# Second-half weights of the attention output projection loaded during attention, into closed tiles' place; row buffers and odd heads' raw query weights share tags

## The chip, the cores and the metric

The kernel runs on one core of one Trainium2 chip. Its engines work at the same time, each through its own instructions in a fixed order, and wait for one another by semaphores: TensorE (PE in the profile; its weight loads PEld), VectorE (DVE), ScalarE (ACT), GpSimd (POOL) and SyncE (SP), which issues most DMA transfers. The metric is the device time of one launch in microseconds.

Before the change the time is 2666.85 us (median of 3 runs, 2663.87 to 2669.19). All stretches below are microseconds from the start of the span of one profiled execution.

## What is computed

One inference step of a two-layer decoder in float32: model width 1024, one prompt of 1024 tokens, and 8 decode sequences of 8 tokens ("samples"). Layer 0 is an S5 state-space mixer and a gated convolutional feed-forward net. Then one shared K and V is projected. Layer 1 is differential attention over it and a second feed-forward net. The part in question:

```
xn = rmsnorm(x, b_pre_g)
q  = (xn @ w_q).reshape(seq, 8 heads, 2, 64)
S_j = softmax(q[:, h, j] @ k[:, h, j].T / 8 + ALiBi bias(h), causal)   # j = 0, 1
o[:, h] = rmsnorm((S_0 - lam * S_1) @ v[:, h], sub_g) * const
x  = x + rmsnorm(o @ w_o, b_post_g)
x  = x + rmsnorm(conv_ffn(rmsnorm(x, f_pre_g)), f_post_g)
```

The samples attend to their own paged past as well. Their scores and values are worked off beside the K and V projection, and their outputs go to a scratch tensor `sod` in device memory.

## The kernel before

Every large product runs in three matmuls: each float32 operand is split into a high and a low part in a fast format, and high*high, low*high and high*low are accumulated (`mm3`, lines 815, 816, 817). A weight is loaded raw by DMA, cast to its high part on ACT (line 798 for the general weights, 1812 for the query weights), and the low part is raw minus high, on DVE (line 799) or POOL (line 1813). An activation is transposed on PE and split by ACT and DVE on the way out of PSUM (lines 150 to 154).

The stages follow one another: S5, its gated output, feed-forward net 0, K/V projection with the samples' attention (`kv_proj`, until about 1462), attention (until about 1801), output projection (`o_proj`, until about 1889) and feed-forward net 1 (to the end). A scheduler orders each engine's instructions over the borders of stages from a model of their times; what is written first does not always come first. Tiles live in pools. A pool that opens where another has closed reuses its bytes, and the first instruction that writes such a tile waits for all instructions that used the old tiles under it.

`attention` has eight heads. `prep(h)` prepares a head: it loads `raw`, the head's 1024x128 piece of w_q (tag `qraw`, one buffer), and `kr`, its keys; multiplies `raw` by the norm's gain on POOL (line 1811), casts it to `qwh` on ACT, subtracts to `qwl` on POOL; makes the bias tile `tb`; transposes the keys into `kh` and `kl` (64 partitions, copied to the other 64 by DMAs that POOL issues, lines 1826 and 1827); and runs 48 matmuls of 512 columns for the queries `qx`. For head 0 the loads of `raw` and `kr` are issued by POOL, for the others by SP. `prep(0)` runs ahead of the loop; the other heads' steps are spread over the loop by the table `STEPS`. In the loop `stage_a` makes scores (lines 1904, 1905), maxima (1907) and exponentials (1911), and `stage_b` combines the two maps (1921), transposes (1929), multiplies by the values (1935) and normalises.

During the last head the rows of `o` come back from scratch (`row_in`, tags `kr` and `row` in turn), are completed with the two last heads' outputs (line 1866), transposed (`row_T`, line 876), and the first half of w_o's columns is multiplied for five of the nine token tiles (`o_half`), with weights in the query and key tiles of even heads. Then `o_proj` loads the second half in four units of 512 KB (`half_units`, `load_w`, lines 793, 798, 799), multiplies it for all nine token tiles (the samples' tile needs the cast at line 976 and uses lines 989, 990), then the first half for the four late tiles. Each finished tile goes through a norm and residual tail (lines 845, 857, 860, 870) that feeds feed-forward net 1.

Of the kernel before, what the change touches and what calls it, by code (L numbers as in the profile page):

```python
# [20 lines left out]
P = 128  # L21
D = 1024
# [51 lines left out]
def trunk_kernel(ctx, tc, I, O):  # L74
# [7 lines left out]
    def nm(s):  # L82
        uid[0] += 1
        return f"{s}_{uid[0]}"
# [679 lines left out]

    def open_w():

        pools["w"] = wstack.enter_context(tc.tile_pool(name="wpool", bufs=1, reuse_waits="tile"))

    def open_dense():

        if "w" not in pools:
            open_w()
        pools["ph"] = wstack.enter_context(tc.tile_pool(name="phase", bufs=1, reuse_waits="tile"))
# [7 lines left out]
    def wslot(name, dtype=F32):  # L781

        c = pools["wc"] = (pools.get("wc", -1) + 1) % NWX
        return pools["w"].tile([P, 1024], dtype, tag=f"wx{c}", name=nm(name), bufs=1)

# [206 lines left out]

    def half_units(wsrc, half, gains=lambda k2: None):
        wv = wsrc.rearrange("(kt p) f -> p kt f", p=P)
        u3 = lambda t: t.rearrange("p (k f) -> p k f", f=512)
        hs = slice(half * 512, half * 512 + 512)
        units = []
        for k2 in range(KT // 2):
            hi, lo = load_w([(u3, wv[:, 2 * k2 : 2 * k2 + 2, hs])], gains(k2))
            units.append((u3(hi), u3(lo)))  # L1000
        return units
# [767 lines left out]
    def attention():  # L1769
        with ExitStack() as ca:  # L1770
            ap1 = ca.enter_context(tc.tile_pool(name="att1", bufs=1, reuse_waits="tile"))
            ap = ca.enter_context(tc.tile_pool(name="att", bufs=1, reuse_waits="tile"))

            def at(shape, tag, bufs=1, dtype=F32, pool=None):
                return (pool or ap).tile(shape, dtype, tag=tag, name=nm(tag), bufs=bufs)
# [20 lines left out]
            def prep(h):  # L1796
# [3 lines left out]
                e = h % 2  # L1800
                raw = at([P, KT, P], "qraw")
                wh = at([P, KT, P], "qwh", 1, F32R)
# [4 lines left out]
                H.update(kh=kh, kl=kl, qx=qx)  # L1807
                dma = (nc.sync if h else GP).dma_start
                dma(raw, wq[:, :, hc])
                dma(kr, kd[0:SEQ, hc].rearrange("(n p) e -> p n e", p=P))  # L1810
                GP.tensor_tensor(raw, raw, bc(bpgc, 2, P), ALU.mult)
# [36 lines left out]
            def row_in(tt):  # L1848

                t0, n = tokens(tt)  # L1850
                t = rows[tt] = at([P, D], ("kr", "row")[tt % 2])
                if tt < NTT:
                    nc.sync.dma_start(t[:, 0 : D - 2 * P], od[t0 : t0 + n, 0 : D - 2 * P])
                    return
                for b in range(NB):

                    src = sod[b].rearrange("(c r) (g e) -> r g c e", r=40, g=2)[0:NQ]
                    dst = t[b * NQ : (b + 1) * NQ].rearrange("q (g c e) -> q g c e", g=2, c=4)
                    for g in range(2):
                        nc.sync.dma_start(dst[:, g], src[:, g])  # L1860
# [102 lines left out]
            for n in range(-LA, len(items)):  # L1963
# [18 lines left out]
                if n == (NH - 1) * NTT:  # L1982
                    row_in(NTT)
                    row_in(NTT - 1)
                if h < NH - 1:
                    stage_b(h, i, *live.pop(n))
                elif i == NTT - 1:
                    row_T(NTT)
                    row_in(i - 1)
                    stage_b(h, i, *live.pop(n))  # L1990
                else:
# [6 lines left out]
                    row_T(i + 1)  # L1998
                    if i:
                        row_in(i - 1)  # L2000
            o_half(1, us, None)
# [4 lines left out]
    def o_proj():  # L2006

        ws = half_units(I["w_o"][0], 1)
        post = row_bcast(I["b_post_g"][0])
# [103 lines left out]
```

## Time and profile before

| | |
|---|---|
| time, median of 3 | 2666.85 us (2663.87 to 2669.19) |
| profiled execution: its time, its span | 2665.99 us, 2664.1 us |
| mean granted TensorE clock | 0.98 of full speed |
| PE busy | 2493.7 us, 94% of the span |
| DVE busy | 1947.8 us, 73% |
| ACT busy | 1281.0 us, 48% |
| POOL busy | 661.2 us, 25% |
| chain that ended last | PE 58%, DVE 13%, DMA 4%, issue 4%, ACT 3%, POOL 3% |

A row of the profile names start, duration, engine (a q behind it marks the engine's DMA or semaphore queue), line, operation, output and inputs, and in brackets how long the engine had stood idle just before and what released it. Here PE is busy nearly everywhere, so what matters are the few places where PE stands idle, or where its granted clock is down after standing.

### The profile page before, as it was taken

What the parts mean: (1) busy time and instruction counts of PE and PEld (TensorE: products, weight loads), DVE (VectorE), ACT (ScalarE), POOL (GpSimd) and SP (SyncE); (2) the same over time, 40 slices, a digit from 0 to 9 for tenths busy, and PEclk for the clock granted to TensorE, in tenths of its full rate; (3) what the DMA queues carried; (4) which work ended last, traced back from release to release, by engine and by line L of the source; (5) the groups of instructions that cost most, each with busy time, mean ns of one, the idle gap of its engine ahead of it and who ended that gap; (6) DMA issues with size and microseconds to landing.
All of it is one profiled execution on the core that took longest, in us unless ns stands there. A gap on an engine that the chain in (4) does not pass through costs nothing.

```text
span 2664.1 us, 39516 instructions
## 1 busy us (share of the span) xinstructions
PE 2493.7 (94%) x14234; PEld 2199.5 (83%) x14234; DVE 1947.8 (73%) x3543; ACT 1281.0 (48%) x2597; POOL 661.2 (25%) x1062
## 2 busy tenths in 40 slices
PE   3778998999999999999999899999899999998997
PEld 2777876999999977788777788877799999996776
DVE  7994358677777789984222688875877777778999
ACT  6763234444444454354322677764544444444433
POOL 3220030111111176501201222113011111127571
PEclk9999998999999999999999899999899999999999
DMA  5443233122222233445646333325322222233334
GB/s 144 104 97 88 84 126 126 58 76 78 85 72 78 81 117 97 125 134 183 207 158 210 104 83 96 98 93 173 127 69 79 75 75 74 75 98 105 92 107 154
DMA packets 265688, 286.77 MB, mean 108 GB/s; under 512 B 42268, under 2 KB 212564, under 8 KB 265492
## 3 DMA queue, kind: packets, MB, share of 16 engines
q1 hardware_dynamic: 261892, 273.55, 33.3%
q0 software_dynamic: 3088, 9.77, 1.7%
q8 instruction: 113, 1.85, 0.3%
q10 hardware_dynamic: 512, 0.92, 0.1%
q14 instruction: 83, 0.68, 0.1%
HBM read 193.58 MB, written 70.93 MB: 99 GB/s over the span
## 4 chain that ended last, share of the span: by engine, by line
PE 58%; DVE 13%; DMA 4%; issue 4%; ACT 3%; POOL 3%; SPq 0%; DVEq 0%; ACTq 0%; POOLq 0%
PE mm L815 17%; PE mm L817 17%; PE mm L816 17%; DVE acc L1437 2%; PE mm L1426 2%; DVE xT_lo L151 2%; DMA gr<-gd 2%; DVE S L1907 1%; ACT S L1911 1%; DVE xT_hi L151 1%; DVE wst L151 1%; PE mm L1935 1%; PE tr L876 1%; DVE acc L860 1%; POOL xr L1306 1%
## 5 line engine op out<-in xcount | busy, mean ns | idle before, releaser
L815 PE MATMUL mm<-xT_hi,whi 128*128 128x384 f32 (+1 forms) x1408 | 457.0, 325 | 2.0 <-ACT acc L1154 1.7
L816 PE MATMUL mm<-xT_lo,whi 128*128 128x384 f32 (+1 forms) x1408 | 456.2, 324 | 1.4 <-DVE xT_lo L151 1.4
L817 PE MATMUL mm<-xT_hi,wlo 128*128 128x384 f32 (+1 forms) x1408 | 454.0, 324 | 0.0
L815 PEld LDWEIGHTS mm<-xT_hi,whi 128*128 128x128 f32 x1408 | 265.4, 189 | 3.8 <-ACT acc L1154 2.4
L816 PEld LDWEIGHTS mm<-xT_lo,whi 128*128 128x128 f32 x1408 | 265.7, 189 | 2.2 <-DVE xT_lo L151 2.1
L817 PEld LDWEIGHTS mm<-xT_hi,wlo 128*128 128x128 f32 x1408 | 265.3, 189 | 0.8
L1203 POOL COPY cvo<-acc 128x2 f32<-128x2 f32 x88 | 54.2, 616 | 814.1 <-ACT acc L1186 814.0
L815 PE MATMUL mm<-whi,xT_hi 128*128 128x512 f32 x608 | 242.9, 404 | 5.8 <-ACT whi L798 5.8
L1200 DVE SCALAR_TENSOR_TENSOR acc<-acc,cpar,acc 128x1104 f32<-128x1104 f32 x176 | 239.9, 1385 | 4.7 <-ACT acc L1198 4.7
L816 PE MATMUL mm<-wlo,xT_hi 128*128 128x512 f32 x608 | 242.8, 400 | 0.1
L817 PE MATMUL mm<-whi,xT_lo 128*128 128x512 f32 x608 | 242.2, 400 | 0.0
L150 ACT CAST whi<-raw 128x1024 fp32r<-128x1024 f32 x88 | 92.7, 1053 | 248.5 <-PE mm L817 245.1
L1437 DVE TENSOR_TENSOR acc<-mm,acc 128x512 f32<-128x512 f32 x279 | 184.3, 679 | 8.4 <-PE mm L817 8.1
L151 DVE TENSOR_TENSOR wlo<-raw,whi 128x1024 fp32r<-128x1024 f32 x88 | 107.7, 1224 | 103.5 <-PE mm L816 90.8
L815 PE MATMUL mm<-acc,whi 128*128 128x384 f32 x528 | 178.8, 339 | 2.5 <-DVE acc L1160 2.5
L817 PE MATMUL mm<-acc,wlo 128*128 128x384 f32 x528 | 178.9, 339 | 0.0
L816 PE MATMUL mm<-acc,whi 128*128 128x384 f32 x528 | 178.3, 338 | 0.0
L815 PEld LDWEIGHTS mm<-whi,xT_hi 128*128 128x128 f32 x608 | 115.3, 190 | 36.9 <-ACT whi L798 6.2
L816 PEld LDWEIGHTS mm<-wlo,xT_hi 128*128 128x128 f32 x608 | 115.2, 189 | 27.9 <-DVE wlo L799 0.8
L817 PEld LDWEIGHTS mm<-whi,xT_lo 128*128 128x128 f32 x608 | 114.9, 189 | 27.9 <-issue 0.8
L1198 ACT ACTIVATE acc<-acc,cpar 128x1104 f32<-128x1104 f32 x88 | 114.2, 1313 | 18.1 <-DVE acc L1169 11.9
L1186 ACT COPY acc<-mm 128x256 f32<-128x256 f32 x88 | 32.4, 369 | 183.7 <-PE mm L817 183.7
(575 smaller groups left out, 6311.6 us busy)
## 6 DMA issues: line engine op xcount, KB each, us to landing
raw<-in_w_up_dram SPq DMA_DIRECT2D x88, 512.0 KB
gd<-acc SPq DMA_DIRECT2D x44, 552.0 KB
raw<-in_w_down_dram SPq DMA_DIRECT2D x44, 512.0 KB
gr<-gd SPq DMA_DIRECT2D x80, 256.0 KB
raw<-in_glu_w_dram SPq DMA_DIRECT2D x40, 256.0 KB
acc<-in_cache_k_dram SPq DMA_DIRECT2D x16, 512.0 KB
acc<-in_cache_v_dram SPq DMA_DIRECT2D x16, 512.0 KB
xj<-in_x_prompt_dram SPq DMA_DIRECT2D x8, 512.0 KB
```

The source lines that it names most:

```text
L150: A.copy(hi_ap, ps_ap)
L151: V.tensor_tensor(lo_ap, ps_ap, hi_ap.bitcast(F32), ALU.subtract)
L815: PE.matmul(out, lh, rh, start=start, stop=False, **kw)
L816: PE.matmul(out, lh, rl, start=False, stop=False, **kw)
L817: PE.matmul(out, ll, rh, start=False, stop=stop, **kw)
L860: V.scalar_tensor_tensor(y[:, hs], y[:, hs], r[0:n], xr[0:n, hs], op0=ALU.mult, op1=ALU.add)
L1186: A.copy(hb[:, 2 + n0 : 2 + SEQ], ps[:, 0:wp])
L1198: A.activation(hc, hb[:, 2 : 2 + TG], AF.Identity, bias=cp[:, ft, 3:4], scale=cp[:, ft, 2:3])
L1200: V.scalar_tensor_tensor(hc, hb[:, tap : tap + TG], cp[:, ft, tap : tap + 1], hc, op0=ALU.mult, op1=ALU.add)
L1203: GP.tensor_copy(co[:, 0:2], hb[:, SEQ : SEQ + 2])
L1426: PE.matmul(pa[h], lt, wt[:, h * 512 : (h + 1) * 512], start=st and j == 0, stop=sp and j == len(seq) - 1)
L1437: V.tensor_tensor(a, ps, a, ALU.add)
```

## The change

It has four parts.

1. The pool of odd heads' tiles (`att1`: their keys, queries, and the bias) moves to the other side of SBUF. The pool of even heads' tiles and of the single tiles (`att`) therefore lies where `att1` lay, and both lie over other closed tiles than before.
2. Odd heads' raw query weights are loaded into the tag `row`, even heads' into `qraw`. Heads 0 and 1's are now issued by POOL, and only head 0's keys.
3. The rows of the end of attention rotate over three tags (`kr`, `row`, `qraw`), and three are asked for at the start of the last head.
4. Three stages before the end of the loop `att1` is closed and the general weight pool opened in its place; two units of w_o's second half are loaded there, a third in the loop's second last step, and only the fourth in `o_proj`. The weight pool is split in two (`wpool` with six of the eleven slots, `wpool2` with five), since only the first fits at that time.

```
-    def open_w():
-
-        pools["w"] = wstack.enter_context(tc.tile_pool(name="wpool", bufs=1, reuse_waits="tile"))
+    def open_w(side="left", more=True):
+
+        if "w" not in pools:
+            pools["w"] = wstack.enter_context(tc.tile_pool(name="wpool", bufs=1, side=side, reuse_waits="tile"))
+            pools["side"] = side
+        if more and "w2" not in pools:
+            pools["w2"] = wstack.enter_context(tc.tile_pool(name="wpool2", bufs=1, side=pools["side"],
+                                                            reuse_waits="tile"))
...
-        return pools["w"].tile([P, 1024], dtype, tag=f"wx{c}", name=nm(name), bufs=1)
+        return pools["w" if c < 6 else "w2"].tile([P, 1024], dtype, tag=f"wx{c}", name=nm(name), bufs=1)
...
-            ap1 = ca.enter_context(tc.tile_pool(name="att1", bufs=1, reuse_waits="tile"))
+
+            ca1 = ExitStack()
+            ap1 = ca1.enter_context(tc.tile_pool(name="att1", bufs=1, side="right", reuse_waits="tile"))
...
-                raw = at([P, KT, P], "qraw")
+                raw = at([P, KT, P], "row" if e else "qraw")
...
-                dma = (nc.sync if h else GP).dma_start
-                dma(raw, wq[:, :, hc])
-                dma(kr, kd[0:SEQ, hc].rearrange("(n p) e -> p n e", p=P))
+
+                (nc.sync if h > 1 else GP).dma_start(raw, wq[:, :, hc])
+                (nc.sync if h else GP).dma_start(kr, kd[0:SEQ, hc].rearrange("(n p) e -> p n e", p=P))
...
-                t = rows[tt] = at([P, D], ("kr", "row")[tt % 2])
+                t = rows[tt] = at([P, D], ("kr", "row", "qraw")[(NTT - tt) % 3])
...
                 if n == (NH - 1) * NTT:
-                    row_in(NTT)
-                    row_in(NTT - 1)
+                    for tt in (NTT, NTT - 1, NTT - 2):
+                        row_in(tt)
+                if n == len(items) - LA:
+                    ca1.close()
+                    open_w("right", False)
+                    first["wo"] = half_units(I["w_o"][0], 1, ks=range(2))
...
-                    row_in(i - 1)
+                    row_in(i - 2)
...
-                    if i:
-                        row_in(i - 1)
+                    if i > 1:
+                        row_in(i - 2)
+                    if i == 1:
+                        first["wo"] += half_units(I["w_o"][0], 1, ks=range(2, 3))
...
-        ws = half_units(I["w_o"][0], 1)
+        ws = first["wo"] + half_units(I["w_o"][0], 1, ks=range(3, 4))
```

Lines behind the edits are numbered 4 to 6 higher than before: 1809 becomes 1815, 1811 is 1817, 1813 is 1819, 1826 is 1832, 798 is 802, 976 is 980, 1887 is 1893, 1866 is 1872.

How the order moves, first on POOL at the start of attention. Before (`qraw_13616` is head 0's raw weight, `qraw_13782` head 1's):

```order
L1784 IOTA tb_13631 128x1024
L1786 AFFINE_SELECT tb_13631<-tb_13631 128x128
L1789 TENSOR_SCALAR tb_13797<-tb_13631 128x1024
L1809 DMA qraw_13616<-in_w_q_dram 128x8x128
L1810 DMA kr_13619<-kd 128x8x128
L1811 TENSOR_TENSOR qraw_13616<-qraw_13616,bpg 128x1024
L1813 TENSOR_TENSOR qwl_13618<-qraw_13616,qwh_13617 128x1024
L1826 DMA kh_2026_13620<-kh_2026_13620 64x1024
```

Of the change (`qraw_13620` is head 0's raw weight, `row_13786` head 1's):

```order
L1815 DMA qraw_13620<-in_w_q_dram 128x8x128
L1816 DMA kr_13623<-kd 128x8x128
L1790 IOTA tb_13635 128x1024
L1815 DMA row_13786<-in_w_q_dram 128x8x128
L1792 AFFINE_SELECT tb_13635<-tb_13635 128x128
L1817 TENSOR_TENSOR qraw_13620<-qraw_13620,bpg 128x1024
L1795 TENSOR_SCALAR tb_13801<-tb_13635 128x1024
L1817 TENSOR_TENSOR row_13786<-row_13786,bpg 128x1024
L1819 TENSOR_TENSOR qwl_13622<-qraw_13620,qwh_13621 128x1024
L1832 DMA kh_2026_13624<-kh_2026_13624 64x1024
```

Head 0's loads move ahead of the bias; the load of head 1's raw weight, two bias operations and head 1's product stand among head 0's three steps. The load of `row_13786` waits for the users of closed `kv_proj` tiles, the last store of sample results (`sod<-acc`) among them.

On ACT in the last steps of attention, of the change (`whi_17437`, `whi_17443`, `whi_17597` are the first three units of w_o's second half; before, no cast of line 798 stands in this stretch):

```order
L1943 ACTIVATE oh_17041<-mm_17387,rl_17382 128x128
L802 CAST whi_17437<-raw_17436 128x1024
L153 ACTIVATE xT_hi<-tr_17357,sgc 128x4x128
L1872 COPY kr_17364<-oh_16548 128x128
L1945 ACTIVATE oj_17400,sso_17040<-oh_17041 128x128
L802 CAST whi_17443<-raw_17442 128x1024
L1936 COPY wt_17454<-tr_17455 128x384
L1872 COPY row_17220<-oh_17041 128x128
L1943 ACTIVATE oh_17041<-mm_17453,rl_17448 128x128
L1945 ACTIVATE oj_17492,sso_17040<-oh_17041 128x128
L153 ACTIVATE xT_hi<-tr_17508,sgc 128x4x128
L802 CAST whi_17597<-raw_17596 128x1024
```

Three casts have moved into attention's last steps, among the copies that the transposes of the rows wait for; DVE has the three subtractions in the same stretch.

On ACT between attention and `o_proj`, before (`oo_17687` is attention's last output, `acc_17807` the samples' high part, `whi_17699` to `whi_17711` the first units):

```order
L1887 COPY oo_17687<-mm_17662 128x512
L976 CAST acc_17807<-xT_hi 128x8x64
L798 CAST whi_17699<-raw_17698 128x1024
L798 CAST whi_17705<-raw_17704 128x1024
L798 CAST whi_17711<-raw_17710 128x1024
```

And of the change (`acc_17814` is the samples' high part, `whi_17724` the fourth unit, `whi_18436` the first unit of the other half):

```order
L1893 COPY oo_17713<-mm_17688 128x512
L802 CAST whi_17724<-raw_17723 128x1024
L802 CAST whi_18436<-raw_18435 128x1024
L980 CAST acc_17814<-xT_hi 128x8x64
L834 ACTIVATE gr_17819,ss_17820<-acc_17817 64x512
```

The samples' cast now stands behind two weight casts. On PE the first product of `o_proj` in either version is the samples' (line 989 before, 993 in the change), which reads that cast; in the change all sixteen of its matmuls stand there, before only one and then other tiles'.

## Rows read from the trace of the kernel before

**Rows 1.** Busy time of the engines by stretch (us; instructions in brackets).

```profile
1440.00:1465.00 25.00, 23.27 (x317) 15.64 (x307) 11.62 (x66) 9.67 (x35) 4.21 (x4) 1.00 0.66 215
1465.00:1500.00 35.00, 25.59 (x110) 20.83 (x108) 20.04 (x60) 14.06 (x37) 12.48 (x12) 0.80 0.60 152
1500.00:1740.00 240.00, 229.04 (x1447) 201.00 (x1446) 208.32 (x671) 190.38 (x518) 58.75 (x43) 1.00 0.33 86
1740.00:1805.00 65.00, 57.45 (x327) 47.13 (x327) 43.45 (x160) 40.85 (x110) 6.78 (x3) 0.97 0.32 104
1805.00:1885.00 80.00, 78.44 (x388) 61.96 (x387) 49.65 (x98) 37.58 (x80) 25.79 (x60) 0.98 0.52 167
1885.00:1905.00 20.00, 12.40 (x53) 10.41 (x52) 19.36 (x48) 12.02 (x31) 2.25 (x4) 0.74 0.44 145
```

**Rows 2.** Timeline of PE at attention's start (start, us, engine, line, operation [idle before]).

```profile
1464.57 0.50 PE L815 MATMUL mm<-xT_hi,qwh 128*128 128x512 f32 x1 [1.24 <-ACT qwh L1812]
1467.19 0.80 PE L817 MATMUL mm<-xT_hi,qwl 128*128 128x512 f32 x1 [1.42 <-POOL qwl L1813]
...
1468.21 0.63 PE L816 MATMUL mm<-xT_lo,qwh 128*128 128x512 f32 x1
...
1479.85 0.40 PE L816 MATMUL mm<-xT_lo,qwh 128*128 128x512 f32 x1
...
1480.32 0.22 PE L1904 MATMUL mm<-kh,qx 128*128 128x128 f32 x1
...
1491.03 0.47 PE L1929 MATMUL tr<-ident,S 128*128 128x128 f32 x1 [7.99 <-DVE S L1921]
```

**Rows 3.** Timeline of POOL, 1390 to 1490.

```profile
1397.25 0.29 POOL L1786 TENSOR_SCALAR_AFFINE_SELECT tb<-tb 128x128 f32<-128x128 f32 x1
1398.79 2.79 POOL L1789 TENSOR_SCALAR tb<-tb 128x1024 f32<-128x1024 f32 x1 [1.24 <-DVE smx L1655]
1452.70 1.00 POOL L1809 DMA_DIRECT2D qraw<-in_w_q_dram  x1 [51.12 <-PE mm L816]
...
1457.63 1.92 POOL L1811 TENSOR_TENSOR qraw<-qraw,bpg 128x1024 f32<-128x1024 f32 x1 [3.04 <-DMA qraw<-in_w_q_dram]
1464.60 2.54 POOL L1813 TENSOR_TENSOR qwl<-qraw,qwh 128x1024 fp32r<-128x1024 f32 x1 [5.05 <-ACT qwh L1812]
...
1483.31 1.89 POOL L1811 TENSOR_TENSOR qraw<-qraw,bpg 128x1024 f32<-128x1024 f32 x1 [11.36 <-DMA qraw<-in_w_q_dram]
```

**Rows 4.** Timeline of SP, 1467 to 1474.

```profile
1468.62 0.32 SPq L1698 DMA_DIRECT2D sod<-acc  x1
1470.51 1.10 SPq L1794 DMA_DIRECT2D v<-vd  x2
1471.73 1.90 SPq L1810 DMA_DIRECT2D kr<-kd  x1
1473.73 3.32 SPq L1809 DMA_DIRECT2D qraw<-in_w_q_dram  x1
```

**Rows 5.** Timeline of DVE, the samples' last norms.

```profile
1464.49 0.42 DVE L1697 TENSOR_TENSOR acc<-acc,rr 128x256 f32<-128x256 f32 x1
1464.84 2.32 DVE L138 TENSOR_TENSOR rs<-rr 128x2 f32<-128x2 f32 x1
1467.19 0.16 DVE L139 TENSOR_TENSOR rs<-rs,rv 128x2 f32<-128x2 f32 x1
...
1468.17 0.42 DVE L1697 TENSOR_TENSOR acc<-acc,rr 128x256 f32<-128x256 f32 x1
```

**Rows 6.** Timeline of ACT, the query weights' casts.

```profile
1463.49 1.03 ACT L1812 CAST qwh<-qraw 128x1024 fp32r<-128x1024 f32 x1
...
1485.24 1.04 ACT L1812 CAST qwh<-qraw 128x1024 fp32r<-128x1024 f32 x1 [7.94 <-POOL qraw L1811]
```

**Rows 7.** Weight casts and subtractions of 1795 to 1825 by line.

```profile
L798 ACT CAST whi<-raw 128x1024 fp32r<-128x1024 f32 x6 | 6.2, 1051 | 10.8 <-DMA raw<-in_w_o_dram 10.8
L799 DVE TENSOR_TENSOR wlo<-raw,whi 128x1024 fp32r<-128x1024 f32 x5 | 6.0, 1224 | 12.7 <-ACT whi L798 12.7
```

**Rows 8.** Busy time, attention's last steps (columns as in Rows 1).

```profile
1770.00:1783.00 13.00, 12.71 (x71) 10.29 (x70) 8.72 (x39) 7.65 (x24) 0.00 (x0) 1.00 0.23 78
```

**Rows 9.** Timeline of PE between attention and the output projection.

```profile
1800.38 0.39 PE L817 MATMUL mm<-qx,xT_lo 128*128 128x512 f32 x1
1802.91 0.50 PE L989 MATMUL mm<-whi,acc 128*128 128x512 f32 x1 [2.14 <-ACT whi L798]
```

**Rows 10.** Timeline of ACT at the same place.

```profile
1801.29 0.62 ACT L976 CAST acc<-xT_hi 128x512 fp32r<-128x512 f32 x1
1801.81 2.00 ACT L798 CAST whi<-raw 128x1024 fp32r<-128x1024 f32 x2
```

**Rows 11.** Timeline of PE between the output projection and feed-forward net 1.

```profile
1894.84 1.94 PE L876 MATMUL tr<-ident,acc 128*128 128x128 f32 x8 [5.85 <-DVE acc L870]
```

**Rows 12.** Waits of PE in 1500 to 1740 (us in total, times, longest).

```profile
PE tr L1929 <- DVE S L1921: 7.2, 10, 1.0
PE tr L1929 <- DVE rl L1919: 2.2, 5, 0.5
```

More of the change, by code (lines that the diff above doesn't have):

```diff
@@ L763, in trunk_kernel @@
     EARLY, LATE = ORDER_O[:5], ORDER_O[5:]
-    def open_w():
-        pools["w"] = wstack.enter_context(tc.tile_pool(name="wpool", bufs=1, reuse_waits="tile"))
+    def open_w(side="left", more=True):
[5 more added lines that the diff above has]
+                                                            reuse_waits="tile"))
     def open_dense():
-        if "w" not in pools:
-            open_w()
+        open_w()
         pools["ph"] = wstack.enter_context(tc.tile_pool(name="phase", bufs=1, reuse_waits="tile"))
@@ L991, in tok_mm, with half_units @@
         return ps
-    def half_units(wsrc, half, gains=lambda k2: None):
+    def half_units(wsrc, half, gains=lambda k2: None, ks=range(KT // 2)):
         wv = wsrc.rearrange("(kt p) f -> p kt f", p=P)
@@ L997, in half_units @@
         units = []
-        for k2 in range(KT // 2):
+        for k2 in ks:
             hi, lo = load_w([(u3, wv[:, 2 * k2 : 2 * k2 + 2, hs])], gains(k2))
```

## Prediction, made before the changed kernel ran

> **What bounds the kernel now.** I read the page first: PE is busy for 94% of the span and leads the chain of waits, so a change to attention can move the end only where PE stands or runs at its lower clock. Second, busy time by stretch [rows 1]. The reader is to see three losses. In 1465 to 1500 PE is busy for 25.6 of 35 us, at a granted clock of 0.80, so part of it at the lower of the two levels (1.2 and 2.4 GHz). In 1740 to 1805 it misses 7.5 us in small pieces. In 1885 to 1905 it misses 7.6 us while DVE is busy for 19.4 of 20 us. In between, 1500 to 1740, it misses 11 us, in waits of at most 1 us for the softmax on DVE [rows 12], and none for a load. Third, the timelines at these places, to see which wait ends last in each.
>
> At the start of attention PE waits 1.24 us for the cast `qwh`, then 1.42 us for `qwl`, runs the other 44 query matmuls from 1467.19 to 1480.32, makes the first scores, and stands 7.99 us until `S` is there [rows 2]. That stall begins with head 1's raw weight: POOL stood 11.36 us until it landed and multiplied it at 1483.31 [rows 3]; ACT, in order, stood 7.94 us until it could cast it at 1485.24 [rows 6]; the first head's exponentials are queued behind that cast. SP had issued the load only at 1473.73 [rows 4], since the single `qraw` was in use by head 0.
>
> **The start of attention.** The change gives head 1's raw weight a tile of its own, and puts its load, its multiplication and two bias operations into POOL's queue ahead of head 0's `qwl`. The load waits for the last store of sample results. Behind it on POOL are head 0's multiplication and `qwl`, and for these wait ACT and PE.
>
> Step 1, when the wait ends. Before, the last store was issued at 1468.62, and the load of `v` that waited for the same tiles at 1470.51 [rows 4], 1.9 us later. Part of the store's lateness is POOL's doing: one 128x2 operation on DVE at 1464.84 took 2.32 us, its like behind it 0.16, and it ended as POOL's `qwl` (1464.60, 2.54 us) did [rows 3, 5]. In the change POOL stands at that moment, so I take off 2.16 us: store 1466.5, wait over at 1468.4.
>
> The Trainium skill, GPSIMD Engine Reference, section "Key points", says that GpSimd shares its SBUF interfaces with VectorE and contends with DVE instructions that have two SBUF inputs, which the slow one has; the trace agrees. By that rule the sum is as given, without it 2.2 us more.
>
> Step 2, head 0. Issue of the load 1.00 us (as for `qraw` at 1452.70), the select 0.29, head 0's multiplication 1.92 [rows 3]: 1471.6. The cast takes 1.03 [rows 6]: the first query matmul at 1472.7 instead of 1464.57, +8.1.
>
> Step 3, `qwl`. POOL goes on with the second bias tile, 2.79 us, to 1474.4, then needs head 1's raw weight. POOL's lone load at 1452.70 had landed at 1457.63, 4.9 us later; SP's, issued at 1473.73 behind three others, was multiplied at 1483.31, 9.6 us later [rows 3, 4]. So it lands between 1473.3 and 1478.0. I take 1475, nearer the first, as it is first in its own queue. Then 1.9 us for its multiplication and 2.5 for `qwl`: 1479.4, where before it was 1467.1: +12.3 us (11.7 to 15.3).
>
> The Trainium skill, DMA: Bandwidth & Descriptors, section "Issuing engines are not separate DMA queues", says that transfers from sync and gpsimd run on the same 16 engines and interleave, so that a second issuer saves only issue time. It speaks against the load's new queue: by it alone I would take the late end, 1478, and the sum would be 3 us higher. The row at 1473.73 agrees with it, the lone load cannot show it.
>
> Step 4, what comes back. The 44 matmuls took 13.1 us, the first at 0.63 us each and the last at 0.40 [rows 2]; after a longer stand I take the same 13.1 (10.3 if all ran like the last). When scores begin, head 1's weight is multiplied already, so ACT casts it at once instead of 4.9 us after the first scores (1485.24 against 1480.32). The 7.99 us stall shrinks by 4.9; the rest is the softmax itself. At best all 8.0 go.
>
> Sum of the start: 12.3 - 4.9 = +7.4 us. Ends: 11.7 - 8.0 - 2.8 = +0.9, and 15.3 - 4.9 = +10.4. PE has no longer stand before 1740 that could swallow this [rows 12]. Later heads' raw weights come a head earlier too, but PE does not wait for them there: 0.
>
> **The end of attention.** Rows in three tags instead of two: the gaps are ACT and DVE chains, not loads, so 0. Three casts of 1.05 us on ACT and three subtractions of 1.22 on DVE [rows 7] now stand in 1770 to 1783, where PE was busy for 12.7 of 13 us, ACT for 7.7 and DVE for 8.7 [rows 8]. Both engines have room, but the casts stand directly ahead of copies that PE's transposes need. Between 0 (all in the gaps) and 3.7 (all three subtractions on the path) I take +1.5. Without the casts' room on ACT it would be the 3.7.
>
> **Between attention and `o_proj`.** Before, PE stands 2.14 us [rows 9], while ACT does the samples' cast (1801.29) and the first weight cast, 1801.81 [rows 10]. Three weights are split early now; but ACT does two others, 2.0 us, ahead of the samples' cast, 0.62, which PE's first product reads. From 1801.29 that is 1803.9, +1.0 us against 1802.91. If ACT reached these two casts earlier it would be -1.5; if their loads came late, +2.
>
> **`o_proj` and after.** From 1805 PE is busy for 78.4 of 80 us [rows 1], so weights that are there earlier give nothing. ACT's 10.8 us of waiting for w_o [rows 7] are its own. The 5.85 us at 1894.84 [rows 11] hang on DVE's chain of norms for late tiles, which follows PE's last products and is only permuted: 0, within 1.5 either way. Feed-forward net 1 is bound by PE: 0.
>
> **Sum.** 7.4 + 1.5 + 1.0 = +9.9 us on the profiled 2665.99: 2675.9. The profiled run is 0.9 us below the median of the three, so on the median it would be 2676.8; I stay with 2675.9. The likeliest case's own range is 2671 to 2681.
>
> **Rivals.** A measurement tells about 0.2% from no change, 5.3 us: 2661.5 to 2672.2.
>
> Not slower, 22%: the early weight of head 1 pays for the start. Place: PE behind the first scores. If the stall goes whole and the query matmuls run at full clock, the start is +0.9, and with 1.5 and 1.0 the time is 2669.4. For it: the stall began with that weight [rows 3, 6]. Against it: exponentials, the combination and DVE's queue remain behind the scores. It decides where less than 1 us is left of the stall.
>
> Faster, 8%: the load of head 1's weight is not held by the store, so POOL's queue flows and only the gains are left: -4.9 at the scores, and -2.1 at `o_proj`'s first product because its weights are there: 2659.0. For it: POOL stood idle for 51 us before 1452.70 [rows 3]. Against it: the order shows the wait, on the last of the samples' tiles.
>
> Much slower, 12%: the load lands at the late end, 1478, beside `v` and `kr`, and the casts at the end are all on the path: 10.4 + 3.7 + 1.0 = +15.1, 2681.1. For it: 9.6 us for the like load [rows 3, 4].
>
> **Chances.** The forecast has 58%, of which 8 may fall within 0.2%. Slower 50 + 12 = 62%; within 20 + 8 = 28%, faster 2 + 8 = 10%. The range 2663 to 2682 takes in the first rival and the third and leaves out the faster one.
>
> **What would show it.** Right: on POOL the load into `row` issued at about 1468.4 after a long idle, `qwl` of head 0 at about 1477, first scores near 1492, and the stall behind them near 3 us. At 1802 of before, moved by about 9 us, PE waits some 3 us for the samples' cast. Wrong: scores before 1486, or a stall as long as before; or PE finding its first product of `o_proj` ready. The forecast falls as a whole if attention's first matmul stays near 1465.

## The result, and the profile after

The changed kernel takes 2673.03 us (median of 20 runs, 2666.43 to 2677.21), the kernel before 2666.03 us on the same chips (20 runs): ratio 1.0027, 95% interval [1.0021, 1.0033], so it is slower by about 7 us. The forecast was 2675.9 us. The profiled execution of after took 2677.21 us (span 2675.4), the slowest of its 20, so I read stretches in it and not its end.

Busy time by stretch after the change, columns as in [rows 1]:

```profile
1465.00:1500.00 35.00, 20.25 (x76) 16.20 (x77) 11.64 (x38) 12.35 (x29) 17.77 (x13) 0.71 0.48 124
1500.00:1740.00 240.00, 229.18 (x1433) 201.12 (x1433) 207.14 (x668) 187.95 (x513) 57.33 (x47) 1.00 0.35 87
1740.00:1805.00 65.00, 57.05 (x341) 48.26 (x340) 53.04 (x178) 44.95 (x120) 6.22 (x3) 0.95 0.35 110
```

PE is busy for 20.25 us of the first 35, where before it was 25.59. Between 1500 and 1740 it is as busy as before (229.18 against 229.04). So I look at attention's start first, in the timelines. POOL's, after:

```profile
1456.74 0.98 POOL L1790 IOTA tb<- 128x1024 f32 x1 [6.51 <-PE mm L1691]
1467.17 0.90 POOL L1815 DMA_DIRECT2D row<-in_w_q_dram  x1 [9.45 <-DMA sod<-acc]
1468.09 0.31 POOL L1792 TENSOR_SCALAR_AFFINE_SELECT tb<-tb 128x128 f32<-128x128 f32 x1
1468.36 1.89 POOL L1817 TENSOR_TENSOR qraw<-qraw,bpg 128x1024 f32<-128x1024 f32 x1
1470.23 2.81 POOL L1795 TENSOR_SCALAR tb<-tb 128x1024 f32<-128x1024 f32 x1
1473.91 1.90 POOL L1817 TENSOR_TENSOR row<-row,bpg 128x1024 f32<-128x1024 f32 x1 [0.87 <-DMA row<-in_w_q_dram]
1475.76 2.34 POOL L1819 TENSOR_TENSOR qwl<-qraw,qwh 128x1024 fp32r<-128x1024 f32 x1
```

The load into `row` stands 9.45 us at the head of POOL's queue until the last store of sample results is over. Behind it are head 0's multiplication, a bias operation, head 1's multiplication (0.87 us more, for its landing), and only then `qwl`, which ends at 1478.1; before, it ended at 1467.1 [rows 3]. PE after, to set beside [rows 2]:

```profile
1453.16 7.47 PE L1691 MATMUL mm<-acc,xr 128*32 128x128 f32 x192
1471.38 0.79 PE L819 MATMUL mm<-xT_hi,qwh 128*128 128x512 f32 x1 [9.73 <-ACT qwh L1818]
1478.16 0.80 PE L821 MATMUL mm<-xT_hi,qwl 128*128 128x512 f32 x1 [4.70 <-POOL qwl L1819]
1490.92 0.22 PE L1910 MATMUL mm<-kh,qx 128*128 128x128 f32 x1
1497.31 0.47 PE L1935 MATMUL tr<-ident,S 128*128 128x128 f32 x1 [3.67 <-DVE S L1927]
```

PE stands 9.73 and 4.70 us, where it was 1.24 and 1.42; the stall behind the first scores is 3.67 us instead of 7.99. The cast of head 1's weight no longer waits for POOL, as it did for 7.94 us in [rows 6]:

```profile
1490.94 1.05 ACT L1818 CAST qwh<-row 128x1024 fp32r<-128x1024 f32 x1 [3.04 <-PE mm L820]
```

Between attention and `o_proj`, ACT after, against [rows 10]: two weight casts now stand ahead of the samples' cast.

```profile
1812.10 0.59 ACT L1893 COPY oo<-mm 128x512 f32<-128x512 f32 x1 [3.46 <-PE mm L821]
1812.58 1.99 ACT L802 CAST whi<-raw 128x1024 fp32r<-128x1024 f32 x2
1814.47 0.62 ACT L980 CAST acc<-xT_hi 128x512 fp32r<-128x512 f32 x1
```

PE after, there and at the end of `o_proj`, against [rows 9] (2.14) and [rows 11] (5.85):

```profile
1815.14 0.80 PE L993 MATMUL mm<-whi,acc 128*128 128x512 f32 x1 [3.08 <-ACT acc L980]
1906.29 1.56 PE L880 MATMUL tr<-ident,acc 128*128 128x128 f32 x8 [3.43 <-DVE rs L136]
```

PE waits 0.94 us longer for its first product of `o_proj`, and 2.4 us less at the end of it.

**Where the time lies, stage by stage.** What comes ahead of attention differs by several us between two profiles of one and the same kernel: the samples' products (row 1453.16 above) begin at 1453.95 in the first profile of before and at 1450.79 in the second, taken later. So I compare lengths of stages, each worked out from four rows of PE like those shown: from the start of the samples' products to the transposes that end the stall behind the first scores (A); on to the first product of `o_proj` with the samples (B); on to the eight transposes that [rows 11] shows (C); on to the end of the span (D).

```
us, one profile each             A      B      C      D     sum    ratio of the medians [95%]
before, first profile          37.1  311.9   91.9  769.3  1210.2
before, second profile (e0)    37.3  315.9   92.3  769.8  1215.3
after                          44.2  317.8   91.2  769.1  1222.2   1.0027 [1.0021, 1.0033]
e1  row's load by SP           46.3  317.1   91.1  769.3  1223.8   1.0031 [1.0018, 1.0043]
e2  no early output weights    44.3  316.8   93.3  769.3  1223.7   1.0029 [1.0017, 1.0040]
e3  no row for head 1          38.8  317.9   89.7  771.1  1217.6   1.0004 [0.9995, 1.0013]
e14 e3, rows in two tags       38.8  314.2   89.7  770.4  1213.0   1.0010 [1.0001, 1.0018]
e6  samples' cast first        45.1  313.4   92.1  768.6  1219.2   1.0024 [1.0014, 1.0033]
e11 low parts on DVE           43.8  316.6   89.0  768.5  1217.9   1.0022 [1.0013, 1.0032]
e12 e1 + product behind qwl    36.5  316.6   89.3  770.7  1213.1   1.0004 [0.9995, 1.0012]
e15 e12 + e6 + e11             37.6  314.6   90.2  766.8  1209.1   0.9984 [0.9975, 0.9993]
e4  before + row for head 1    36.8  318.8   91.0  772.7  1219.3   1.0021 [1.0011, 1.0031]
e10 e4 + product behind qwl    33.8  315.8   91.8  770.0  1211.3   0.9990 [0.9981, 0.9998]
e13 e10 + low parts on DVE     33.8  316.4   91.5  770.2  1211.9   0.9992 [0.9981, 1.0003]
```

Between the second profile of before and that of after, A gains 6.9 us, B 1.9, C loses 1.1 and D 0.7: +6.9, as the medians say. Each figure is of one profile. Two profiles of the kernel before differ by 4 us in B (the next section says why), so a difference of 1 us in a single stage tells little. The chips differ by some us too (before has 2663.2 to 2666.0 us on them), so below each time stands as its distance from before on the same chip, for after +7.0.

### The profile page after: what moved, and what is told of

Its sections match the earlier page's. It is cut to its first block, busy times and chain, and to the rows that moved or that the text cites. A ratio compares the mean times of both kernels' runs of the same rounds, so it can differ in the third digit from the quotient of the medians.

```text
span 2675.4 us, 39554 instructions
## 1 busy us (share of the span) xinstructions
PE 2495.7 (93%) x14234; PEld 2202.9 (82%) x14234; DVE 1944.0 (73%) x3543; ACT 1277.3 (48%) x2597; POOL 622.1 (23%) x1063
## 4 chain that ended last, share of the span: by engine, by line
PE 58%; DVE 14%; DMA 3%; issue 3%; ACT 3%; POOL 3%; SPq 0%; DVEq 0%; POOLq 0%; ACTq 0%
PE mm L819 17%; PE mm L821 16%; PE mm L820 16%; DVE acc L1441 2%; PE mm L1430 2%; DVE xT_lo L151 2%; DVE S L1913 1%; DMA gr<-gd 1%; ACT S L1917 1%; DVE xT_hi L151 1%; PE mm L1941 1%; DVE wst L151 1%; DVE S L1927 1%; DMA raw<-in_w_up_dram 1%; DVE acc L864 1%
## 5 line engine op out<-in xcount | busy, mean ns | idle before, releaser
L1207 POOL COPY cvo<-acc 128x2 f32<-128x2 f32 x88 | 47.4, 538 | 843.3 <-ACT acc L1190 843.2
L1913 DVE CUSTOM_DVE_ANT_0 S<-mm,tb 128x512 f32<-128x512 f32 (+3 forms) x192 | 101.1, 551 | 22.6 <-PE mm L1911 19.3
```

What stands on the lines that cost most here:

```text
L1207: GP.tensor_copy(co[:, 0:2], hb[:, SEQ : SEQ + 2])
L1913: V.tensor_tensor_reduce(S_[j][:, k0 : k0 + w], ps[:, 0:w], H["tb"][:, b0 : b0 + w], 0.125, -3e38, ALU.add, ALU.max, mx[:, j, c : c + 1])
```

## The experiments

### A wait that before itself sometimes has

Between the two profiles of before, B differs by 4 us, so before anything else this had to be understood. Kernel before again, unedited (e0).

> The kernel before, unchanged, for a second profile: how far two profiles of one program differ by stage. In 1737 to 1750 of the first profile of before, attention runs 3.9 us shorter than in that of the change, where a DVE operation on S took 2.88 us instead of 1.14 beside a POOL subtraction. If that is a race that either kernel may win or lose, the second profile may show it here too; if the change brings it about, this stretch is within 0.5 us of the first profile's. Stages before 1400 may differ by up to 5 us, as they do between the profiles seen so far. Time 2662 to 2670.

It took 2667.89 us in its one run. The first profile of before, DVE and then POOL (timelines, 1725 to 1745):

```profile
1728.23 1.15 DVE L1921 SCALAR_TENSOR_TENSOR S<-S,cc,S 128x896 f32<-128x896 f32 x1
1733.04 1.28 DVE L1921 SCALAR_TENSOR_TENSOR S<-S,cc,S 128x1024 f32<-128x1024 f32 x1
1741.20 1.14 DVE L1921 SCALAR_TENSOR_TENSOR S<-S,cc,S 128x896 f32<-128x896 f32 x1
...
1733.43 3.14 POOL L1879 TENSOR_TENSOR kh<-qraw,kh 128x1024 fp32r<-128x1024 f32 x1 [5.66 <-ACT kh L1878]
1741.78 2.81 POOL L1879 TENSOR_TENSOR kl<-qraw,kl 128x1024 fp32r<-128x1024 f32 x1 [5.21 <-ACT kl L1878]
```

The second profile, the same operations, and PE behind them:

```profile
1726.53 1.15 DVE L1921 SCALAR_TENSOR_TENSOR S<-S,cc,S 128x896 f32<-128x896 f32 x1
1731.34 3.32 DVE L1921 SCALAR_TENSOR_TENSOR S<-S,cc,S 128x1024 f32<-128x1024 f32 x1
1741.03 2.90 DVE L1921 SCALAR_TENSOR_TENSOR S<-S,cc,S 128x896 f32<-128x896 f32 x1
...
1731.13 2.44 POOL L1879 TENSOR_TENSOR kh<-qraw,kh 128x1024 fp32r<-128x1024 f32 x1 [5.06 <-PE mm L1935]
1740.59 2.39 POOL L1879 TENSOR_TENSOR kl<-qraw,kl 128x1024 fp32r<-128x1024 f32 x1 [7.02 <-ACT kl L1878]
...
1745.29 0.63 PE L1929 MATMUL tr<-ident,S 128*128 128x128 f32 x4 [2.85 <-DVE xT_lo L154]
```

Whichever of the two engines starts first runs at its own speed (DVE 1.28, POOL 2.4 us), and the other stands until it is done: POOL's 2.44 us from 1731.13 end at 1733.57, and 1.28 us later is 1734.85; DVE's long operation ended at 1734.66, within 0.2 us of that. When POOL wins, PE waits 2.85 us, for `xT_lo`, which stands behind `S` on DVE; in the first profile there is no such wait. In the 11 profiles of kernels with these operations on POOL it won 9 times, in that of after too (DVE's 128x1024 and 128x896 took 3.30 and 2.88 us); DVE won in the first profile of before and in that of e14. So the 4 us by which the first profile of before looks shorter in B are not the change's: 2.8 of them lie between the first row of each view above and the first product of `o_proj`, the other 1.2 in the heads ahead of it. The Trainium skill, SBUF — State Buffer, section "SBUF: two separate sides", says of the pair of ports that the two engines share that whichever instruction starts first has it to its end and the other blocks; the rows agree.

### Which part costs the start

**e3: the change without its second part** (head 1's raw weight in `qraw`, loaded by SP).

```
-                raw = at([P, KT, P], "row" if e else "qraw")
-                (nc.sync if h > 1 else GP).dma_start(raw, wq[:, :, hc])
+                raw = at([P, KT, P], "qraw")
+                (nc.sync if h else GP).dma_start(raw, wq[:, :, hc])
```

> The change without part 2: one tag qraw for all heads' raw query weights, head 1's issued by SP; pools, rows in three tags and early output weights as in the change. My theory: the load that waits for the samples' last store is gone from POOL's queue, but the order there now has the copies of kh and kl ahead of qwl, and the bias behind 1457: first query matmul 1465 to 1468, qwl near 1472, first scores near 1485, and the stall of 8 us stays: 5 us above before at 1737, 8 in the end, 2672 to 2674. Rival (all the start's loss is part 2's): start as before, only the 2 to 3 us at the end of attention remain, 2667 to 2669.

Measured: 2665.99 us, 1.0004 [0.9995, 1.0013], +1.8 us where after has +7.0; A is 38.8. My theory, 2672 to 2674, was wrong, and the rival was right about whose loss it is: the second part costs the start, as the forecast had it. PE and then ACT, e3:

```profile
1465.50 0.80 PE L819 MATMUL mm<-xT_hi,qwh 128*128 128x512 f32 x1 [8.10 <-ACT qwh L1818]
1468.37 0.79 PE L821 MATMUL mm<-xT_hi,qwl 128*128 128x512 f32 x1 [0.79 <-POOL qwl L1819]
1487.74 0.43 PE L1935 MATMUL tr<-ident,S 128*128 128x128 f32 x1 [3.67 <-DVE S L1927]
...
1463.20 1.18 ACT L150 CAST kh<-tr 64x512 fp32r<-64x512 f32 x2 [4.57 <-DVE kl L151]
1464.40 1.04 ACT L1818 CAST qwh<-qraw 128x1024 fp32r<-128x1024 f32 x1
```

Against my working, the stall is 3.67 us here too, with no early weight for head 1. The scores are later by themselves (ACT casts `qwh` behind `kh`, and PE waits 8.10 us for it), so the weight is there in time. The scores come 6.0 us later than in the second profile of before, and 4.5 of these come back in the stall, 8.20 us there.

**e4: the second part alone**, in the kernel before, where `row` does not lie on the samples' tiles (the same two lines the other way).

> The kernel before with part 2 of the change alone: odd heads' raw query weights in the tag row, heads 0 and 1's issued by POOL; pools, rows and output weights as before. Here the row tile lies over tiles whose last user is a matmul that ended at 1457.4, not over the last stored one. My theory: POOL is not held, head 0 starts as before (first query matmul 1464.6 to 1466, first scores 1480 to 1482), and the stall of 8.0 us behind the scores shrinks to about 3 to 4: 4 to 5 us faster than before, 2661 to 2662. Rival (an early raw weight costs head 0 through POOL's queue wherever it lies): first scores at 1485 or later, time 2668 or more. Second rival (the stall is the softmax and not the weight): the stall stays near 8 us, 2666.

Measured: 2671.26 us, +6.4, 1.0021 [1.0011, 1.0031]; a miss. The load is issued at once, and the stall is 3.51 us, as expected, but A is 36.8, no loss and little gain: head 1's multiplication stands on POOL between head 0's and `qwl`, head 0's keys come late, and the scores wait 0.68 and 2.79 us for their copies. POOL and then PE, e4:

```profile
1454.80 0.88 POOL L1808 DMA_DIRECT2D row<-in_w_q_dram  x1 [3.12 <-PE mm L1687]
1460.43 1.93 POOL L1810 TENSOR_TENSOR row<-row,bpg 128x1024 f32<-128x1024 f32 x1 [2.83 <-DMA row<-in_w_q_dram]
1462.33 2.33 POOL L1812 TENSOR_TENSOR qwl<-qraw,qwh 128x1024 fp32r<-128x1024 f32 x1
1469.44 0.55 POOL L1826 DMA_DIRECT2D kl<-kl  x1 [4.25 <-DVE kl L151]
...
1480.51 0.33 PE L1904 MATMUL mm<-kl,qx 128*128 128x128 f32 x1 [2.79 <-DMA kl<-kl]
```

What e4 loses lies in B (318.8) and D (772.7); its cause was not found.

**e10: e4 with head 1's multiplication behind head 0's `qwl`.** Head 1 multiplies by a copy of the gain to which zero times a piece of `qwl` is added, so the two cannot change places. Head 2's is tied in the same way to head 1's multiplication, but not to head 1's `qwl`.

```
+                g = heads[h - 1]["g"] if 0 < h < 3 else bpgc
-                GP.tensor_tensor(raw, raw, bc(bpgc, 2, P), ALU.mult)
+                GP.tensor_tensor(raw, raw, bc(g, 2, P), ALU.mult)
+                if h < 2:
+                    z, H["g"] = at([P, KT], "bpz"), at([P, KT], f"bpg{h}")
+                    GP.tensor_scalar(z, raw[:, 0, 0:KT] if h else wl[:, 0, 0:KT].bitcast(F32), 0.0, None, op0=ALU.mult)
+                    GP.tensor_tensor(H["g"], bpgc, z, ALU.add)
```

> The kernel before with head 1's raw weight in the tag row, issued early by POOL (as in the last but one run, e4), and with head 1's multiplication by the gain made to wait for head 0's qwl, by a gain tile that is computed from it (bpg plus 0 times qwl), so that on POOL it stands behind head 0's copies. My theory (in e4 POOL's multiplication for head 1 at 1460 held DVE's small operations for the samples and so head 0's kl, whose copies the scores then waited for): scores and their transposes no longer wait for kh and kl, first scores within 1 us of before, the stall behind them 3 to 4 us instead of 8: 4 to 5 us faster than before up to 1737, time 2660 to 2663 if nothing later takes it back. Rival (the stall is the copies' landing or the softmax): the stall stays above 6 us, 2665 or more.

Measured: 2661.52 us, 0.9990 [0.9981, 0.9998]: faster than before by 2.6 us, where e4 is slower by 6.4. The time is as expected, the way to it is not: the stall is 6.37 us and not 3 to 4, as the rival had it. PE, e10:

```profile
1464.35 0.50 PE L817 MATMUL mm<-xT_hi,qwl 128*128 128x512 f32 x1 [1.27 <-POOL qwl L1813]
1484.77 0.47 PE L1933 MATMUL tr<-ident,S 128*128 128x128 f32 x1 [6.37 <-DVE S L1925]
```

A is 33.8, 3.5 under the second profile of before. Of this, 2.5 us are the query matmuls, which run here at the higher clock. Busy time from the first product with `qwl` to the first scores (columns as in [rows 1]), e10 and then the second profile of before:

```profile
1464.35:1474.71 10.36, 10.36 (x45) 8.37 (x45) 5.59 (x15) 2.32 (x4) 4.88 (x9) 1.00 0.83 184
1464.30:1477.19 12.89, 12.89 (x45) 10.29 (x46) 5.10 (x12) 2.33 (x4) 2.07 (x4) 0.78 0.90 201
```

e13, below, has 10.37 us at 1.00 too. What decides that clock is not shown: PE stood 1.24 and 1.27 us just ahead of these matmuls in e10, and 0.60 and 0.55 in the second profile of before.

The stall stays long although ACT casts head 1's weight 0.04 us after the first scores. POOL's order bites again, one head later. POOL and then DVE, e10:

```profile
1480.36 1.90 POOL L1811 TENSOR_TENSOR qraw<-qraw,bpg 128x1024 f32<-128x1024 f32 x1 [7.89 <-DMA qraw<-in_w_q_dram]
1482.21 2.35 POOL L1813 TENSOR_TENSOR qwl<-row,qwh 128x1024 fp32r<-128x1024 f32 x1
1482.32 2.40 DVE L1925 SCALAR_TENSOR_TENSOR S<-S,cc,S 128x128 f32<-128x128 f32 x1
```

Head 1's `qwl` stands behind head 2's multiplication, which waits 7.89 us for its own load. DVE's combination, 0.34 us in the profiles of before and after, starts 0.11 us behind `qwl` and takes 2.40; PE's transposes wait for it. e4 and e13 have the same order on POOL; a kernel with head 2's multiplication behind head 1's `qwl` was not run. So it is not shown that the early weight by itself shortens the start. What e10 shows is that the place of head 1's multiplication on POOL is worth 9.0 us against e4, 3.0 of them in A; the rest lies in B and D, where e4's loss is open.

**e1: the changed kernel, `row` loaded by SP.** One line: `(nc.sync if h else GP).dma_start(raw, ...)`.

> The change, with one word undone: head 1's raw query weight is issued by SP again, not by POOL. My theory (what costs is the place in POOL's in-order queue that waits for the samples' last store, not who issues the load): POOL now waits at the multiplication itself, which stands ahead of head 0's, so head 0 is held even longer, until the load has landed (about 1474 instead of 1467). First query matmul near 1479 (the change 1471.4), first scores near 1496 (1490.9), time 5 us above the change, about 2678, 12 above before. Rival (the load on POOL's queue is what costs, and SP's is better): first query matmul near 1465 to 1468, time 2666 to 2668.

Measured: 2672.62 us, +7.7, about as after. POOL waits where my theory said, but the time is not 5 us above after's; the rival's early first matmul did not come either. POOL, e1:

```profile
1467.46 1.90 POOL L1817 TENSOR_TENSOR row<-row,bpg 128x1024 f32<-128x1024 f32 x1 [14.30 <-DMA row<-in_w_q_dram]
```

POOL no longer waits to issue, and waits 14.30 us in the next instruction that needs the load, with `qwl` behind it as before. PE's first product waits 15.51 us.

**e12: e1 with e10's edit** (both holds taken from POOL's queue ahead of head 0).

> The changed kernel with two edits: SP issues head 1's raw load, and a data dependence places head 1's multiplication behind head 0's qwl on POOL. Theory (the start's loss is two holds in series on POOL ahead of head 0's qwl, the issue that waits for the last sample store and the multiplication that waits for the landing; either alone is enough to hold it): first query matmul near 1465, qwl without a long wait, the stall behind the first scores about 6 us, the start 0 to 3 us shorter than before, and the time 6 to 8 us under the changed kernel: 2665 to 2667 beside a before of 2664 to 2666. Rival (where the samples' tiles and att1 lie costs the start by itself, whoever issues): first matmul stays at 1471 or later and the time at 2670 or more.

Measured: 2664.40 us, +1.2, 1.0004 [0.9995, 1.0012], where e1 has +7.7 and after +7.0; A is 36.5, 9.8 under e1. SP issues the load at 1463.53, behind the last stores. PE and then POOL, e12:

```profile
1458.87 0.50 PE L819 MATMUL mm<-xT_hi,qwh 128*128 128x512 f32 x1 [2.33 <-ACT qwh L1819]
1466.18 0.80 PE L821 MATMUL mm<-xT_hi,qwl 128*128 128x512 f32 x1 [5.68 <-POOL qwl L1820]
1484.52 0.47 PE L1940 MATMUL tr<-ident,S 128*128 128x128 f32 x1 [3.67 <-DVE S L1932]
...
1463.20 0.55 POOL L1838 DMA_DIRECT2D kl<-kl  x1 [4.53 <-DVE kl L151]
1463.78 2.35 POOL L1820 TENSOR_TENSOR qwl<-qraw,qwh 128x1024 fp32r<-128x1024 f32 x1
```

The first query matmul comes 10.8 us after the start of the samples' products, as in before (10.6 and 10.9), where it is 18.2 in after and 24.0 in e1. So the loss of the start is that POOL waits for head 1's load ahead of head 0's work. Two details are not as expected: `qwl` still comes late (PE waits 5.68 us), since on POOL the copies of head 0's keys now stand ahead of it and that of `kl` waits 4.53 us for DVE; and the stall, 3.67 us and not 6, pays for that. The time is 0.6 us under the expected range. Whether the issue alone would still hold it, with the multiplication moved, was not tried.

### The end of attention and the boundary

**e2: the changed kernel without early output weights** (`ws = half_units(I["w_o"][0], 1)` in `o_proj`, none in attention).

> The change without part 4: the second half of w_o is asked for in o_proj as before, in a pool opened after attention. My theory: the start keeps its loss of about 6 us; the casts leave the last steps of attention (1.0 to 1.5 us) and the samples' cast stands ahead of the weight casts again (1.0 us): about 2 us below the change, 2671. Rival (the early weights are worth their name at o_proj's first product): the time rises by 2 us or more above the change, 2675.

Measured: 2672.54 us, +7.7, about as after; neither expected time came. PE's wait at the boundary is 2.14 us again, and B is shorter by 1.0, as that wait is; the three casts leave no other mark in B. What is won is lost in C (93.3 against 91.2).

**e6: the samples' cast first in `o_proj`** (`xsx = sample_pair()` one block up).

> The change, with the samples' cast written ahead of the fourth weight unit in o_proj, so that ACT does it first. My theory: PE's wait at o_proj's first product falls from 3.1 to about 1.2 us, 1.9 us below the change, about 2671. Rival (the wait only moves to a weight cast or its low part, or is taken back by the norms behind o_proj): within 0.5 us of the change, 2673.

Measured: 2671.66 us, +6.8, 1.0024 [1.0014, 1.0033]: nothing that can be told from after, as the rival had it. The wait alone is as my theory said; PE, e6:

```profile
1807.00 0.50 PE L993 MATMUL mm<-whi,acc 128*128 128x512 f32 x1 [1.19 <-ACT acc L980]
1899.08 1.94 PE L880 MATMUL tr<-ident,acc 128*128 128x128 f32 x8 [7.94 <-DVE acc L874]
```

But where PE comes 1.9 us earlier out of the boundary, it stands 7.94 us at the end of `o_proj` instead of 3.43. There DVE's chain of norms ends last.

**e14: e3 with the rows in two tags, as before.**

> The changed kernel without the row tile for head 1's raw weight (2666.0 when run, +2 us at the end of attention in its profile) and with the rows in two tags as before; only the pools and the early output weights are left. Theory (the three row tags move DVE's and ACT's work at the end of attention and cost the 2 us): the stretch to 1786 as before and 2663.5 to 2664.5, the same as before. Rival (the three early casts and subtractions, or the pool that closes, cost it): stays at 2665.5 to 2666.5.

Measured: 2665.31 us, +2.1, 1.0010 [1.0001, 1.0018], beside 1.0004 for e3: my theory was wrong, and the third tag costs nothing that shows. What is left, the pools and the early weights, is still some 2 us over before; A, 38.8 against 37.3, has 1.5 of it. Its shorter B comes from the race above, which DVE won (1.29 and 1.15 us for the operations that took 3.30 and 2.88).

**e11: the late output low parts on DVE** (`OWG = 0`), and **e13: the same in e10.**

> The change, with the four subtractions for the first half of w_o on DVE (1.22 us each) instead of POOL (2.4 us each). My theory (the change lost 3.9 us in 1740 to 1750 because POOL's subtraction began before DVE's long operation and held it): no operation of line 1927 is longer than 1.3 us there, and the stretch gets back 1 to 3 us, with the DVE's own 4.9 us partly on the path: 2670 to 2672. Rival (DVE is the bound in that stretch anyway and pays all four): 2 to 5 us above the change, 2675 to 2678.

> The kernel before with head 1's raw weight in row and its multiplication behind head 0's qwl (2661.5 when run), and the late output low parts on DVE in place of POOL. Theory (POOL's 128x1024 subtractions hold DVE's S operations near 1737 to 1749, and the low parts on DVE end that): no S operation on DVE of 2.5 us or more there, 1 to 2 us under 2661.5: 2659.5 to 2660.5. Rival (the time is only passed on to DVE, which is in PE's way just as much): 2661 to 2662.

Measured: e11 2671.02 us, +6.9, 1.0022 [1.0013, 1.0032]; e13 2662.44 us, -0.8, 0.9992 [0.9981, 1.0003]. DVE's operations on `S` are short in both (1.28 and 1.14), so the race is gone, yet e11 is no faster than after, and e13 no faster than e10 (-2.6): DVE now does the low parts itself, which is the likely reason but was not tested apart. e11 lies in its expected range only because before is 1.9 us faster on that chip; e13 came nearer to its rival.

**e15: all three mends together** (e12, e6 and e11).

> The changed kernel with all three mends: load by SP and multiplication behind head 0's qwl, the samples' cast first in o_proj, the late output low parts on DVE. Theory (the mends add up, -6 to -8 at the start, -1 to -1.5 at the boundary, -1 to -2 near 1745): 2662 to 2665, faster than before by 0 to 3 us at most. Rival (the later two are covered once the start is earlier): as the kernel with the first mend alone, within 0.7 us of it.

Measured: 2658.73 us, 0.9984 [0.9975, 0.9993]: 4.5 us under before and 5.7 under e12 on the same chip, where after is 7.0 over before. It is the fastest of all kernels here, ahead of e10 (-2.6), and beats both kernels of this case; both expectations were too slow. The two later mends bring more on top of e12 (5.7) than I expected (2 to 3.5), though e6, e11 and e13 gained nothing with one of them; in the one profile 2.1 of it lies in B and 3.9 in D, and the latter I can't explain.

## Why the prediction was right, and where its sum was off

The direction and the mechanism of the loss were right; the reason given for what comes back was not. The forecast of +9.9 us was 2.9 over the +7.0 measured. By its terms:

- **Step 1, the wait.** I said 1468.4 for the load's issue, and it was 1467.17; the samples' products began 0.8 us earlier in that profile, so the miss is 0.4 us. That it is so small is partly luck. SP issued the last store at 1464.81, where I said 1466.5: before, POOL had held a second DVE operation of the samples' norms, which the working left out (the last section has its row). And the wait behind the store was 2.4 us, not 1.9.
- **Steps 2 and 3.** First query matmul: said 1472.7, was 1471.38. Landing: I chose 1475, the multiplication began at 1473.91, again 0.3 us apart with the shift. Ready `qwl`: said 1479.4, was 1478.1. From issue to multiplication the load took 6.7 us, between the lone load's 4.9 and SP's 9.6, as chosen (6.6); the late end of 1478 was not reached.
- **Step 4, what comes back.** Stall: said 4.9 us less, measured 4.3 (7.99 to 3.67). The size was right, the reason was not: e3 and e14 show the same 3.67 without the early weight, and e4, e10 and e13, with it and with scores no later than before's, take 11.4, 10.1 and 10.5 us from the first scores to the transposes, where before takes 10.7 and 10.9. In after the scores come 11.4 us late; e3 gets the same back with 6.0 us and no early weight. The reading behind the step was wrong too: the single `qraw` was free when its last reader, `qwl`, ended at 1467.1 [rows 3]; the load was issued only at 1473.73 because it stood in SP's queue behind the last store, `v` and `kr` [rows 4]. The query matmuls took 12.8 us (1478.16 to 1490.92) against 13.1; the 10.3 at full clock, which the rows named for it do not give, is what e10 and e13 measured.
- **Sum of the start.** Said +7.4; A says +7.1 and +6.9 against the two profiles of before, and with its cause taken away the medians lose 5.8 (e12, from +7.0 to +1.2) and 5.2 (e3, to +1.8).
- **Casts in attention's end.** Said +1.5. B is 1.9 longer than in the second profile of before, 0.9 of it the boundary. The rest, 1.0, is there without the casts too (e2). So the casts cost nothing that shows, the lower end of my range. What makes the 1.0, within the spread of single profiles, stays open.
- **Boundary.** Said +1.0, was +0.94 (2.14 to 3.08).
- **`o_proj` and after.** Said 0, since the chain of norms there is only permuted. PE's wait there fell by 2.4 us, C by 1.1 and D by 0.7: with the casts, this is the term that is off most. A wait for another engine's chain can take up what comes late ahead of it; e2 and e6 point the same way, with less wait at the boundary and a longer C, or 7.94 us of wait. I should have taken the boundary's +1.0 off again there, from the 5.85 us of [rows 11]. With single profiles this stays an argument.
- **Waits in 1500 to 1740.** Said at most 1 us. The view of [rows 12] has one more, of 1.4 us, for ACT's `wt`; nothing in the sum hangs on it.

Of the rivals: "not slower" needed the stall to go whole, and 3.5 to 6.4 us stayed in every kernel with head 1's weight in time, where the rival wanted less than 1. "Faster" needed the load not to be held, and it stood 9.45 us. "Much slower" needed the late landing. That the time could be had back by order alone, which none of the rivals says, is what e12 and e10 show.

## What to carry to other kernels

A load that is asked for early is early only if its buffer is free: look up what lies under the new tile, and what stands behind the waiting instruction on its engine. Moving the issue to another queue does not help while the first consumer stands in the same place; put the consumer behind the work that is due first, and look at the next load's consumer in the same queue as well. And before a stretch is read as the change's, profile the old kernel twice.

## What the runs showed of the hardware

The race between DVE and POOL was the surprise: a lead of 0.1 to 0.2 us can decide which of two operations waits out the other, DVE's 128x1024 (1.28 or 3.3 us) or POOL's (2.4 or 3.1 to 3.4), and with it whether PE stands 2.9 us. At the samples' norms it showed once more, unasked: a 128x2 operation took 2.32 us in [rows 5] beside POOL's `qwl`, and another 1.75 us beside POOL's multiplication, which began at 1457.63 and took 1.92 [rows 3]. DVE, before:

```profile
1457.82 1.75 DVE L139 TENSOR_TENSOR rs<-rs,rv 128x2 f32<-128x2 f32 x1
```

In after, where POOL stood at that time, all of them took 0.15 to 0.17.
